# A two-layer decoder trunk: layer 1's adaLN vectors as row sums on VectorE over transposed weights

## The chip, the cores and the metric

The kernel runs on one core of a Trainium2 chip. The metric is the device time of one execution in microseconds (us), as the median of several runs. The core's engines are named as in its profile: PE (TensorE matmul), PEld (TensorE weight load), DVE (VectorE), ACT (ScalarE), POOL (GpSimd), and SP, whose queue issues nearly all DMAs.

## The reference

Two layers work on x of 256 tokens by 2048 features, in float32. Layer 0 mixes with a convolution module, layer 1 with differential attention; each is followed by a squared-ReLU MLP of width 8192. Each layer is steered by six vectors of 2048, the adaLN vectors, that come from one conditioning vector c:

```python
cond = jax.nn.silu(c)                            # (1, 2048)
for i in range(2):
    mod = cond @ ada_w[i] + ada_b[i]             # ada_w[i]: (2048, 6 * 2048)
    sh_m, sc_m, g_m, sh_f, sc_f, g_f = jnp.split(mod, 6, axis=-1)
    h = x * (1.0 + sc_m) + sh_m
    y = conformer_conv(h, ...) if i == 0 else diff_attention(h, ...)
    x = layer_norm(alpha * x + g_m * y, ln_mix_g[i], ln_mix_b[i])
    h = x * (1.0 + sc_f) + sh_f
    y = jnp.square(relu(h @ mlp_w1[i] + mlp_b1[i])) @ mlp_w2[i] + mlp_b2[i]
    x = layer_norm(alpha * x + g_f * y, ln_ffn_g[i], ln_ffn_b[i])
```

The weights `ada_w` are two matrices of 2048 by 12288 floats, 201 MB together, each element used once.

## The kernel before, in words

All large products are done in tiles of 512 output columns. A weight tile `w` of 1 MB (4 blocks of 128 rows by 512 columns) comes by one DMA from SP's queue into a ring of four buffers (`wraw`, tag "raw"). In two halves of 128x1024, ACT rounds it to fp32r (`wh`, line 629) and DVE takes the rest (`wl`, line 631); each 128x512 block of weights is then multiplied three times for each of two token halves on PE (lines 669, 671 and 672). A weight tile is thus 24 matmuls, two ACT casts and two DVE subtractions. ACT, DVE, PE and SP each work their queue in order, so a late `wl` stops PE, and a DVE instruction that waits holds up every `wl` behind it.

The adaLN vectors that this change touches are the last 12 of 16 column blocks of layer 0's last vector (`G_F`, gate of the MLP) and all six of layer 1. They are made during layer 0's MLP and layer 1, spread between weight tiles by `pump_slow`: a table `marks` says how many steps shall have been issued after so many weight tiles. The first 16 steps go between tiles 3 and 17, 66 more up to tile 122, some in the attention, 8 in the output projection `wo`, the last 8 at tiles 196 to 207.

A step (`ada_steps`, line 373) loads 128 rows of `ada_w` by 2048 columns (1536 for layer 0's) into a buffer of the same ring as the weight tiles, and DVE adds it, times one cond value for each partition, to the accumulator `acc` (lines 377 and 379). After 16 steps, `acc` holds 128 partial sums for each column. Four steps of the order's clock (`SUM_WAIT`) later PE adds them over the partitions with a block of ones (line 387, `adps`: four matmuls, three for layer 0's), ACT copies the result (line 390, `adrow`), PE turns it into columns with four transposes (line 396, `adpt`), and DVE adds the bias (line 399) into `mod`, which is 128 partitions by 16.

Layer 0's `G_F` is wanted soon after: `gate_bcast` turns `mod` into rows on PE (`gbm_p`), writes them to DRAM (`gbm_d`) and reads them back over all partitions (`gbm`, 1 MB), for the first product `w2g` on DVE (line 839) in the MLP's second matrix.

The pools of the early part are closed (`close_early`) about when the first step is issued; `acc` lies in a pool, `late`, that opens there. The order within each engine is set by a scheduler that goes by priorities, with a hand-made order on some engines in the early part.

Of the kernel before, what the change touches and what calls it, by code (L numbers as in the profile page):

```python
# [29 lines left out]
DEPTH = 2  # L30
# [11 lines left out]
ADA_MLP = 66  # L42
ADA_WO = 8
# [7 lines left out]
M2 = (196, 207)  # L51
M1 = (3,17)
# [3 lines left out]
ACT_Q = (0,2)  # L56
SUM_WAIT = 4
COL_WAIT = 1
POOL_T2 = ((5,),(2,5),(2,5),())
# [9 lines left out]
SH_M, SC_M, G_M, SH_F, SC_F, G_F = range(6)  # L69
# [4 lines left out]
MAGIC = 1.5 * 2.0 ** 23  # L74
PI_IN = 3.1415925


@with_exitstack
def trunk(
# [19 lines left out]
    late = {}  # L99
# [4 lines left out]
    def tp_tile(name):  # L104
        return ps_tp[0].tile([P, 512], F32, tag="tp", name=name)
# [65 lines left out]
    def defer(n, fn):  # L171
        put_off.append((ticks[0] + n, fn))
# [14 lines left out]
    adab = []  # L187
# [178 lines left out]

    def ada_steps(i, v, q0=0, m=None):

        st = {}
        c0, nr = q0 * NG, 32 * (4 - q0)  # L370

        def step(kc):
            w = wraw.tile([P, 2048], F32, tag="raw", name=f"adaw_{i}_{v}_{kc}")[:, c0:]
            nc.sync.dma_start(w, ada_w[i, kc * P:(kc + 1) * P, v * D + c0:(v + 1) * D])
            if kc == 0:
                st["acc"] = late["pool"].tile([P, D], F32, tag="acc", name=f"acc_{i}_{v}")[:, c0:]
                nc.vector.tensor_scalar(st["acc"], w, cond[:, 0:1], None, ALU.mult)
            else:
                nc.vector.scalar_tensor_tensor(  # L379
                    st["acc"], w, cond[:, kc:kc + 1], st["acc"], ALU.mult, ALU.add)  # L380
            if kc == KC - 1:
                st["m"] = m or mod_tile(i, v)

                def sums():
# [4 lines left out]
                    rows = work.tile([P, NG], F32, tag="bc_b2", name=f"adrow_{i}_{v}", bufs=1)  # L389
                    nc.scalar.copy(rows[:nr, :], ps[:nr, :])  # L390
                    defer(COL_WAIT, lambda: columns(rows))

                def columns(rows):
                    pt = tp_tile(f"adpt_{i}_{v}")
                    for j in range(4):
                        nc.tensor.transpose(out=pt[:, j * P:j * P + nr], in_=rows[:nr, j * P:(j + 1) * P],
                                            identity=ident[:nr, :nr])
                    for q in range(q0, 4):
                        nc.vector.tensor_tensor(st["m"][:, 4 * q:4 * q + 4],
                                                pt.rearrange("p (j n) -> p j n", j=4)[:, :, 32 * (q - q0)],  # L400
                                                adab[i][:, v * KC + 4 * q:v * KC + 4 * q + 4], op=ALU.add)
                    mods[(i, v)] = st["m"]
                defer(SUM_WAIT, sums)
        return [lambda kc=kc: step(kc) for kc in range(KC)]


# [1434 lines left out]
```

## Time and profile before

| | us |
|---|---|
| median of 3 runs | 2349.42 |
| lowest and highest run | 2344.43 and 2352.29 |
| span of the profiled execution, first to last instruction | 2342.9 |
| PE busy in that span | 2279.1 (97%) |
| DVE busy | 1743.6 (74%) |
| ACT busy | 1089.7 (47%) |
| DMA | 606.50 MB, mean 259 GB/s |

The profiled execution's own time is known by its span alone; what lies around the span is not listed. The span is 1.5 us below the lowest of the three runs and 6.5 us below their median. Busy time on PE counts a matmul that waits inside its pipeline as well, so that 97% is not 97% of PE's best; how close its instructions start behind one another tells more.

### The profile page before, as it was taken

To read this page: it belongs to the slowest core of one execution; us is meant where nothing else is said; L and a number is where in the kernel's file an instruction comes from. 1 tells how busy PE (TensorE), PEld (TensorE's weight loads), DVE (VectorE), ACT (ScalarE), POOL (GpSimd) and SP (SyncE) were. 2 spreads that over 40 slices of the span, in tenths; PEclk is the share of its full clock that TensorE was granted. 3 is DMA by queue.
4 is the path that set the end of the run, shared out by engine and by line. 5 is a ranking of instruction groups with operands and counts; after the bars stand their busy time and mean duration, and the time that the engine had idled before them with its cause. 6 is when DMAs were issued, how large, how long until landed. Compare 5 with 4: busy or idle time off the path is not lost.

```text
span 2342.9 us, 28838 instructions
## 1 busy us (share of the span) xinstructions
PE 2279.1 (97%) x11265; PEld 1809.2 (77%) x11265; DVE 1743.6 (74%) x2031; ACT 1089.7 (47%) x1503; POOL 149.4 (6%) x110
## 2 busy tenths in 40 slices
PE   7999989999999999999999999999999999999999
PEld 4676647777788888888878888877888888888886
DVE  5787788878887888877878876887975655655566
ACT  3344674365345445445454454545443443443442
POOL 0000002002200000000004200010220000000000
PEclk9999999999999999999999999999999999999999
DMA  9998489869988888888847655784876565555563
GB/s 342 377 341 295 164 314 376 316 221 329 326 315 308 312 290 307 308 301 291 310 163 269 242 201 195 256 319 162 305 247 202 180 197 191 187 186 193 189 223 108
DMA packets 264721, 606.50 MB, mean 259 GB/s; under 512 B 11137, under 2 KB 24583, under 8 KB 251527
## 3 DMA queue, kind: packets, MB, share of 16 engines
q1 hardware_dynamic: 264472, 604.62, 73.9%
q8 instruction: 88, 1.44, 0.3%
q14 instruction: 49, 0.39, 0.0%
q10 hardware_dynamic: 112, 0.05, 0.0%
HBM read 602.48 MB, written 2.15 MB: 258 GB/s over the span
## 4 chain that ended last, share of the span: by engine, by line
PE 74%; issue 16%; DVE 6%; ACT 2%; DMA 2%; POOL 0%; POOLq 0%; ACTq 0%; DVEq 0%; SPq 0%
PE w_ps L669 18%; PE w_ps L671 18%; PE w_ps L672 18%; DVE wl_w L631 1%; DMA w_w<-in_mlp_w_dram 1%; PE pw_ps L669 1%; PE qkv_v_ps L672 1%; PE qkv_v_ps L669 1%; PE qkv_v_ps L671 1%; PE qkv_q_ps L672 1%; PE qkv_q_ps L669 1%; DVE acc L379 1%; PE qkv_q_ps L671 1%; PE pw_ps L671 1%; PE pw_ps L672 1%
## 5 line engine op out<-in xcount | busy, mean ns | idle before, releaser
L631 DVE TENSOR_TENSOR wl_w<-w_w,wh_w 128x1024 fp32r<-128x1024 f32 x510 | 633.3, 1259 | 340.0 <-ACT wh_w L629 339.3
L629 ACT CAST wh_w<-w_w 128x1024 fp32r<-128x1024 f32 x512 | 537.0, 1054 | 703.4 <-PE w_ps L672 563.9
L669 PE MATMUL w_ps<-wh_w,hm_hi 128*128 128x512 f32 x1024 | 402.3, 393 | 3.0 <-ACT hm_hi L490 3.0
L671 PE MATMUL w_ps<-wl_w,u_hi 128*128 128x512 f32 x1024 | 399.4, 390 | 4.1 <-DVE wl_w L631 4.1
L671 PE MATMUL w_ps<-wl_w,hm_hi 128*128 128x512 f32 x1024 | 399.5, 390 | 2.5 <-DVE wl_w L631 2.5
L672 PE MATMUL w_ps<-wh_w,hm_lo 128*128 128x512 f32 x1024 | 399.3, 390 | 1.6 <-DVE hm_lo L493 1.6
L669 PE MATMUL w_ps<-wh_w,u_hi 128*128 128x512 f32 x1024 | 400.6, 391 | 0.0
L672 PE MATMUL w_ps<-wh_w,u_lo 128*128 128x512 f32 x1024 | 399.1, 390 | 0.0
L379 DVE SCALAR_TENSOR_TENSOR acc<-adaw,cond,acc 128x2048 f32<-128x2048 f32 (+1 forms) x105 | 244.5, 2329 | 0.1
L669 PEld LDWEIGHTS w_ps<-wh_w,hm_hi 128*128 128x128 f32 x1024 | 192.5, 188 | 47.5 <-ACT hm_hi L490 4.5
L671 PEld LDWEIGHTS w_ps<-wl_w,u_hi 128*128 128x128 f32 x1024 | 192.4, 188 | 45.3 <-DVE wl_w L631 5.8
L671 PEld LDWEIGHTS w_ps<-wl_w,hm_hi 128*128 128x128 f32 x1024 | 192.5, 188 | 43.4 <-DVE wl_w L631 4.6
L672 PEld LDWEIGHTS w_ps<-wh_w,hm_lo 128*128 128x128 f32 x1024 | 192.4, 188 | 43.0 <-DVE hm_lo L493 3.1
L669 PEld LDWEIGHTS w_ps<-wh_w,u_hi 128*128 128x128 f32 x1024 | 192.6, 188 | 42.0 <-issue 1.7
L672 PEld LDWEIGHTS w_ps<-wh_w,u_lo 128*128 128x128 f32 x1024 | 192.5, 188 | 40.2
L580 PE MATMUL pw_ps<-wh_pw,h_hi 128*128 128x512 f32 x256 | 105.7, 413 | 9.4 <-DVE sums L1122 3.3
L581 PE MATMUL pw_ps<-wl_pw,h_hi 128*128 128x512 f32 x256 | 101.5, 397 | 5.1 <-DVE wl_pw L569 5.1
L582 PE MATMUL pw_ps<-wh_pw,h_lo 128*128 128x512 f32 x256 | 100.8, 394 | 0.0
L569 DVE TENSOR_TENSOR wl_pw<-w_pw,wh_pw 128x1024 fp32r<-128x1024 f32 x64 | 77.5, 1220 | 21.2 <-ACT wh_pw L568 21.2
L568 ACT CAST wh_pw<-w_pw 128x1024 fp32r<-128x1024 f32 x64 | 65.8, 1050 | 41.6 <-PE pw_ps L582 24.5
L580 PEld LDWEIGHTS pw_ps<-wh_pw,h_hi 128*128 128x128 f32 x256 | 48.5, 190 | 39.5 <-issue 16.1
L581 PEld LDWEIGHTS pw_ps<-wl_pw,h_hi 128*128 128x128 f32 x256 | 48.7, 190 | 15.9 <-DVE wl_pw L569 7.2
(375 smaller groups left out, 3147.4 us busy)
## 6 DMA issues: line engine op xcount, KB each, us to landing
w_w<-in_mlp_w_dram SPq DMA_DIRECT2D x256, 1024.0 KB, 5.4
adaw<-in_ada_w_dram SPq DMA_DIRECT2D x96, 1024.0 KB, 5.6
aw<-in_ada_w_dram SPq DMA_DIRECT2D x40, 1024.0 KB, 7.3
w_pw<-in_conv_pw_w_dram SPq DMA_DIRECT2D x64, 512.0 KB, 9.1
conv_ux<-in_ada_w_dram SPq DMA_DIRECT2D x17, 1024.0 KB, 12.9
w_pw<-in_conv_pw_w_dram SPq DMA_DIRECT2D x16, 1024.0 KB, 9.2
w_qkv_q<-in_attn_qkv_w_dram SPq DMA_DIRECT2D x16, 1024.0 KB, 5.4
w_qkv_k<-in_attn_qkv_w_dram SPq DMA_DIRECT2D x16, 1024.0 KB, 5.2
```

What stands on the lines that cost most here:

```text
L379: nc.vector.scalar_tensor_tensor(st["acc"], w, cond[:, kc:kc + 1], st["acc"], ALU.mult, ALU.add)
L568: nc.scalar.copy(hq, rq)
L569: nc.vector.tensor_tensor(lq, rq, hq.bitcast(F32), op=ALU.subtract)
L580: nc.tensor.matmul(pss[t], lhsT=xh, rhs=wh, start=(kc == first), stop=False)
L581: nc.tensor.matmul(pss[t], lhsT=xh, rhs=wl, start=False, stop=False)
L582: nc.tensor.matmul(pss[t], lhsT=xl, rhs=wh, start=False, stop=(kc == last))
L629: nc.scalar.copy(hi, rq)
L631: eng.tensor_tensor(lo, rq, hi.bitcast(F32), op=ALU.subtract)
L669: nc.tensor.matmul(pss[tt], lhsT=xh, rhs=wh, start=(kc == 0 and job["bias"] is None), stop=False)
L671: nc.tensor.matmul(pss[tt], lhsT=xh, rhs=wl, start=False, stop=False)
L672: nc.tensor.matmul(pss[tt], lhsT=xl, rhs=wh, start=False, stop=(kc == nk - 1))
```

## The change

The weights of these vectors are laid out anew, transposed and in chunks, before the kernel is launched: a new input `ada_rows` holds, for each column block `ch`, a chunk of 128 output columns by 2048 inputs. A step now loads one chunk (1 MB, one piece of memory, rows of 8 KB) and makes 128 finished values with one DVE instruction: chunk times cond, summed along the row into one column of `mod`. For that, cond must lie on every partition as a row of 2048: it is computed once more in row form at the start (`cond_r`, 16x128, one ACT and one DVE instruction), written to DRAM (`cond_mem`, from ACT's queue), and read back to all partitions (`cond_rows`, 1 MB) when the pool `late` opens, in the place that `acc` had. The product is written over the chunk in place. Layer 0's part is 12 steps of 2048 wide in place of 16 of 1536; the others keep 16 steps. The sums, copies and transposes (lines 387, 390 and 396), both waits, and the bias adds in fours go; one bias add for each vector stays.

```diff
+ADA_ROWS = {key: n for n, key in enumerate([(0, G_F, ch) for ch in range(4, KC)] + [
+    (1, v, ch) for v in range(6) for ch in range(KC)])}
...
+    cond_r = work.tile([P, P], F32, tag="S", name="cond_r", bufs=3)[:KC, :]
+    nc.scalar.activation(cond_r, c_rows, AF.Sigmoid)
+    nc.vector.tensor_tensor(cond_r, cond_r, c_rows, op=ALU.mult)
+    cond_mem = dram.tile([KC, P], F32, tag="cond", name="cond_mem")
+    nc.scalar.dma_start(cond_mem, cond_r)
...
-        def step(kc):
-            w = wraw.tile([P, 2048], F32, tag="raw", name=f"adaw_{i}_{v}_{kc}")[:, c0:]
-            nc.sync.dma_start(w, ada_w[i, kc * P:(kc + 1) * P, v * D + c0:(v + 1) * D])
-            if kc == 0:
-                st["acc"] = late["pool"].tile([P, D], F32, tag="acc", name=f"acc_{i}_{v}")[:, c0:]
-                nc.vector.tensor_scalar(st["acc"], w, cond[:, 0:1], None, ALU.mult)
-            else:
-                nc.vector.scalar_tensor_tensor(
-                    st["acc"], w, cond[:, kc:kc + 1], st["acc"], ALU.mult, ALU.add)
...
-                    ps = tp_tile(f"adps_{i}_{v}")
-                    for q in range(q0, 4):
-                        nc.tensor.matmul(ps[32 * (q - q0):32 * (q - q0) + 32, :], lhsT=ones[:, 0:32],
-                                         rhs=st["acc"][:, q * NG - c0:(q + 1) * NG - c0], start=True, stop=True)
...
+        def step(ch):
+            w = wraw.tile([P, D], F32, tag="raw", name=f"adaw_{i}_{v}_{ch}")
+            nc.sync.dma_start(w, ada_rows[ADA_ROWS[i, v, ch]])
...
+            nc.vector.scalar_tensor_tensor(w, w, 1.0, late["cond"], ALU.mult, ALU.mult,
+                                           accum_out=st["m"][:, ch:ch + 1])
+            if ch == KC - 1:
+                mf = st["m"][:, ch0:]
+                nc.vector.tensor_tensor(mf, mf, adab[i][:, v * KC + ch0:(v + 1) * KC], op=ALU.add)
...
+        late["cond"] = late["pool"].tile([P, D], F32, tag="acc", name="cond_rows")
+        with tc.issue_after(raws["dma"].ins):
+            nc.sync.dma_start(late["cond"], cond_mem.rearrange("k p -> (k p)").partition_broadcast(P))
...
-        marks = ((0, 0), (M1[0], 0), (M1[1], 16), (122, 16 + ADA_MLP), (133, 16 + ADA_MLP))
+        marks = ((0, 0), (M1[0], 0), (M1[1], 12), (122, 12 + ADA_MLP), (133, 12 + ADA_MLP))
```

Three places show what moves. The first is PE at the end of a layer-1 vector in layer 0's MLP; `w_0_1_2_ps` is the sum of a weight tile's product. Before:

```order
L672 MATMUL w_0_1_2_ps_5864<-wh_w_0_1_2_2_1_5925,hm_lo 128x512
L387 MATMUL adps_1_5997<-acc_1_4930,ones 32x512 x4
L669 MATMUL w_0_1_2_ps_5863<-wh_w_0_1_2_3_0_5947,hm_hi 128x512
L671 MATMUL w_0_1_2_ps_5863<-wl_w_0_1_2_3_0_5948,hm_hi 128x512
```

Now:

```order
L656 MATMUL w_0_1_2_ps_5845<-wh_w_0_1_2_2_1_5906,hm_lo 128x512
L653 MATMUL w_0_1_2_ps_5844<-wh_w_0_1_2_3_0_5928,hm_hi 128x512
L655 MATMUL w_0_1_2_ps_5844<-wl_w_0_1_2_3_0_5929,hm_hi 128x512
L656 MATMUL w_0_1_2_ps_5844<-wh_w_0_1_2_3_0_5928,hm_lo 128x512
```

The sums are gone, and so are the transposes at seven like places; the order of the instructions that stay on PE is the same.

The second place is SP's queue where the first steps are issued. Before:

```order
L618 DMA w_w_0_0_1_0_4221<-in_mlp_w_dram 128x4x512
L374 DMA adaw_5_0_4253<-in_ada_w_dram 128x1536
L374 DMA adaw_5_1_4257<-in_ada_w_dram 128x1536
L618 DMA w_w_0_0_1_1_4272<-in_mlp_w_dram 128x4x512
L374 DMA adaw_5_2_4300<-in_ada_w_dram 128x1536
```

Now:

```order
L602 DMA w_w_0_0_1_0_4226<-in_mlp_w_dram 128x4x512
L379 DMA adaw_5_4_4260<-in_ada_rows_dram 128x2048
L1475 DMA cond_rows<-cond_mem 128x2048
L602 DMA w_w_0_0_1_1_4275<-in_mlp_w_dram 128x4x512
L379 DMA adaw_5_5_4303<-in_ada_rows_dram 128x2048
```

The read of `cond_rows`, which takes no buffer of the ring, stands where the second step's load stood.

The third place is SP's queue at the start of layer 0's second MLP matrix, where the gate `gbm` is read back. Before:

```order
L787 DMA gbm_d<-gbm_r 16x128
L374 DMA adaw_1_2_5070<-in_ada_w_dram 128x2048
L825 DMA basem_d<-basem_r 16x128
L618 DMA w_w_0_0_1_2_5085<-in_mlp_w_dram 128x4x512
L788 DMA gbm_4986<-gbm_d 128x2048
L618 DMA w_w_0_0_1_3_5123<-in_mlp_w_dram 128x4x512
```

Now:

```order
L771 DMA gbm_d<-gbm_r 16x128
L379 DMA adaw_1_2_5051<-in_ada_rows_dram 128x2048
L809 DMA basem_d<-basem_r 16x128
L772 DMA gbm_4967<-gbm_d 128x2048
L602 DMA w_w_0_0_1_2_5066<-in_mlp_w_dram 128x4x512
L602 DMA w_w_0_0_1_3_5104<-in_mlp_w_dram 128x4x512
```

The gate's read has moved ahead of one weight tile's load.

## Rows read from the trace of the kernel before

**Rows 1.** From the page: PE's busy time, share and instructions, and PE's granted clock in 40 equal slices of the span, in tenths.

```profile
PE 2279.1 (97%) x11265; PEld 1809.2 (77%) x11265; DVE 1743.6 (74%) x2031; ACT 1089.7 (47%) x1503; POOL 149.4 (6%) x110
...
PEclk9999999999999999999999999999999999999999
```

**Rows 2.** The table by stage: from and to, length, busy time of PE, PEld, DVE, ACT and POOL with the number of instructions, granted clock, DMA share, GB/s.

```profile
500.00:560.00 60.00, 57.93 (x264) 47.23 (x263) 49.28 (x35) 33.27 (x59) 11.90 (x6) 1.00 0.89 316
560.00:620.00 60.00, 55.75 (x245) 43.51 (x244) 47.37 (x39) 26.46 (x38) 14.25 (x6) 0.97 0.90 329
620.00:1195.00 575.00, 575.00 (x2604) 473.20 (x2603) 459.30 (x435) 269.80 (x362) 6.52 (x4) 1.00 0.85 303
...
1275.00:1525.00 250.00, 249.46 (x1163) 204.94 (x1162) 191.21 (x271) 126.66 (x231) 38.90 (x39) 1.00 0.66 225
1525.00:1600.00 75.00, 73.20 (x325) 59.65 (x325) 62.33 (x70) 31.81 (x42) 6.32 (x4) 1.00 0.80 284
...
1640.00:1715.00 75.00, 74.55 (x349) 60.50 (x348) 69.89 (x60) 34.30 (x40) 18.52 (x8) 1.00 0.89 303
```

**Rows 3.** The timeline of PE around one vector's sums and transposes: start, time, engine, line, operation.

```profile
725.53 0.39 PE L672 MATMUL w_ps<-wh_w,hm_lo 128*128 128x512 f32 x1
725.85 1.07 PE L387 MATMUL adps<-acc,ones 128*32 128x512 f32 x8
726.84 0.50 PE L669 MATMUL w_ps<-wh_w,hm_hi 128*128 128x512 f32 x1
727.18 0.39 PE L671 MATMUL w_ps<-wl_w,hm_hi 128*128 128x512 f32 x1
...
729.47 0.39 PE L672 MATMUL w_ps<-wh_w,hm_lo 128*128 128x512 f32 x1
729.71 0.60 PE L396 MATMUL adpt<-ident,adrow 128*128 128x128 f32 x4
...
730.37 0.40 PE L671 MATMUL w_ps<-wl_w,hm_hi 128*128 128x512 f32 x1
```

**Rows 4.** The chain of work that ended last, in order of time (start, time, what): the pieces of the sums, six in all, of which the first and the last.

```profile
725.91 1.00 PE adps L387 x8
...
1701.65 1.00 PE adps L387 x8
```

**Rows 5.** Groups of instructions on DVE and ACT, forms apart: line, engine, operation, out<-in, shapes, count, busy us, mean ns of one, idle before.

```profile
L379 DVE SCALAR_TENSOR_TENSOR acc<-adaw,cond,acc 128x2048 f32<-128x2048 f32 x90 | 214.2, 2380 | 0.0
L377 DVE TENSOR_SCALAR acc<-adaw,cond 128x2048 f32<-128x2048 f32 x6 | 7.7, 1282 | 4.0 <-PE adps L387 4.0
L399 DVE TENSOR_TENSOR mod<-adpt,cols_adab 128x4 f32<-128x4 f32 x27 | 2.5, 152 | 1.7 <-PE adpt L396 1.7
L1457 DVE SCALAR_TENSOR_TENSOR r<-r 128x512 f32<-128x512 f32 x32 | 22.2, 692 | 1.1
L1772 DVE SCALAR_TENSOR_TENSOR z<-z,lnf_rs,fin 128x512 f32<-128x512 f32 x5 | 3.8, 752 | 0.2
...
L1653 ACT ACTIVATION_READ_ACCUMULATOR at_sm<-at_sm,at_mx 128x1 f32 x32 | 6.0, 187 | 0.0
```

**Rows 6.** The table by stage, for the instructions of line 379 alone: from and to, length, DVE busy with the number of instructions, granted clock, DMA share, GB/s.

```profile
620.00:1195.00 575.00, 135.85 (x58) 1.00 0.85 303
...
1640.00:1715.00 75.00, 20.83 (x8) 1.00 0.89 303
```

**Rows 7.** The chain of work that ended last: the pieces of the steps, 13 of line 379, of which the first and the last, and the one of line 377.

```profile
509.27 0.53 DVE acc L379
...
582.57 1.20 DVE acc L377
...
1688.66 2.26 DVE acc L379
```

**Rows 8.** The timeline of DVE and of PE around the gate's read (in brackets the idle time before and what ended it), and the table by stage for the same place.

```profile
600.21 0.69 DVE L839 TENSOR_TENSOR w2g<-w_ps,gbm 128x512 f32<-128x512 f32 x1 [5.43 <-DMA gbm<-gbm_d]
...
603.01 1.22 DVE L631 TENSOR_TENSOR wl_w<-w_w,wh_w 128x1024 fp32r<-128x1024 f32 x1
...
604.28 0.50 PE L671 MATMUL w_ps<-wl_w,u_hi 128*128 128x512 f32 x1 [2.40 <-DVE wl_w L631]
...
609.79 0.50 PE L671 MATMUL w_ps<-wl_w,u_hi 128*128 128x512 f32 x1 [1.28 <-DVE wl_w L631]
...
604.00:612.00 8.00, 6.44 (x22) 4.71 (x23) 8.00 (x6) 1.04 (x1) 4.66 (x2) 0.79 0.82 264
```

**Rows 9.** The DMA issues (KB each, median us from issue to landing) of the two reads over all partitions that have one, SP's queue and DVE at the first steps, and a stretch with the DMA engines full.

```profile
conv_ux<-gb_d SPq DMA_DIRECT2D x1, 1024.0 KB, 12.5
gba<-gba_d SPq DMA_DIRECT2D x1, 1024.0 KB, 6.6
...
471.23 14.16 SPq L374 DMA_DIRECT2D adaw<-in_ada_w_dram  x2
...
493.68 1.01 DVE L377 TENSOR_SCALAR acc<-adaw,cond 128x1536 f32<-128x1536 f32 x1
...
572.00:580.00 8.00, 7.61 (x37) 5.09 (x36) 3.85 (x5) 7.57 (x14) 0.00 (x0) 1.00 1.01 375
```

**Rows 10.** The timeline of PE: behind the sums of layer 0's vector, and at the start of the kernel.

```profile
576.03 0.50 PE L671 MATMUL w_ps<-wl_w,u_hi 128*128 128x512 f32 x1 [0.39 <-DVE wl_w L631]
...
7.45 1.94 PE L327 MATMUL aps_b<-aw_bNone,condr 128*32 128x256 f32 x16 [4.34 <-DMA aw_bNone<-in_ada_w_dram]
```

More of the change, by code (lines that the diff above doesn't have):

```diff
@@ L56 @@
 ACT_Q = (0,2)
-SUM_WAIT = 4
-COL_WAIT = 1
 POOL_T2 = ((5,),(2,5),(2,5),())
@@ L84, in trunk @@
     conv_pw2_w, conv_pw2_b, attn_qkv_w, attn_lq1, attn_lk1, attn_lq2, attn_lk2,
-    attn_subln_g, attn_o_w, mlp_w1, mlp_b1, mlp_w2, mlp_b2, inv_freq, out,
+    attn_subln_g, attn_o_w, mlp_w1, mlp_b1, mlp_w2, mlp_b2, inv_freq, ada_rows, out,
 ):
@@ L365, in ada_both_steps, with ada_steps @@
         return la, lb, [lambda a=a: step(a) for a in range(n_pairs)], finish
-    def ada_steps(i, v, q0=0, m=None):
+    def ada_steps(i, v, ch0=0, m=None):
         st = {}
-        c0, nr = q0 * NG, 32 * (4 - q0)
-        def step(kc):
-            w = wraw.tile([P, 2048], F32, tag="raw", name=f"adaw_{i}_{v}_{kc}")[:, c0:]
-            nc.sync.dma_start(w, ada_w[i, kc * P:(kc + 1) * P, v * D + c0:(v + 1) * D])
-            if kc == 0:
-                st["acc"] = late["pool"].tile([P, D], F32, tag="acc", name=f"acc_{i}_{v}")[:, c0:]
-                nc.vector.tensor_scalar(st["acc"], w, cond[:, 0:1], None, ALU.mult)
-            else:
-                nc.vector.scalar_tensor_tensor(
-                    st["acc"], w, cond[:, kc:kc + 1], st["acc"], ALU.mult, ALU.add)
-            if kc == KC - 1:
-                st["m"] = m or mod_tile(i, v)
-                def sums():
-                    ps = tp_tile(f"adps_{i}_{v}")
-                    for q in range(q0, 4):
-                        nc.tensor.matmul(ps[32 * (q - q0):32 * (q - q0) + 32, :], lhsT=ones[:, 0:32],
-                                         rhs=st["acc"][:, q * NG - c0:(q + 1) * NG - c0], start=True, stop=True)
[L389 to L404, printed above, removed]
@@ new lines, in step @@
+        def step(ch):
+            w = wraw.tile([P, D], F32, tag="raw", name=f"adaw_{i}_{v}_{ch}")
+            nc.sync.dma_start(w, ada_rows[ADA_ROWS[i, v, ch]])
+            if ch == ch0:
+                st["m"] = m or mod_tile(i, v)
+            nc.vector.scalar_tensor_tensor(w, w, 1.0, late["cond"], ALU.mult, ALU.mult,
[3 more added lines that the diff above has]
+                nc.vector.tensor_tensor(mf, mf, adab[i][:, v * KC + ch0:(v + 1) * KC], op=ALU.add)
+                mods[(i, v)] = st["m"]
@@ L407, in trunk @@
+        return [lambda ch=ch: step(ch) for ch in range(ch0, KC)]
     ada_q, items, n_items, limit, after_load = [], [], [0, 0], [5], []
@@ L466, in trunk @@
     gf_load, gf_use = ada_slice_steps(0, G_F, 0, 4, m_gf, apart=True)
-    ada_q.extend(ada_steps(0, G_F, 1, m_gf))
+    ada_q.extend(ada_steps(0, G_F, 4, m_gf))
     for iv in [(1, SC_M), (1, SH_M), (1, G_M), (1, SC_F), (1, SH_F), (1, G_F)]:
@@ L1488, in close_early @@
         late["pool"] = ctx.enter_context(tc.tile_pool(name="late", bufs=1))
-    n_ada0 = 7 * KC
+        late["cond"] = late["pool"].tile([P, D], F32, tag="acc", name="cond_rows")
+        with tc.issue_after(raws["dma"].ins):
+            nc.sync.dma_start(late["cond"], cond_mem.rearrange("k p -> (k p)").partition_broadcast(P))
+    n_ada0 = 6 * KC + 12
     tiles_done = [0]
@@ L1496, in pump_slow @@
         n = tiles_done[0]
-        marks = ((0, 0), (M1[0], 0), (M1[1], 16), (122, 16 + ADA_MLP), (133, 16 + ADA_MLP))
+        marks = ((0, 0), (M1[0], 0), (M1[1], 12), (122, 12 + ADA_MLP), (133, 12 + ADA_MLP))
         left = 80 - ADA_MLP
         for g in range(4):
-            marks += ((133 + 12 * g, 96 - left * (4 - g) / 4), (137 + 12 * g, 96 - left * (3 - g) / 4))
-        marks += ((177, 96), (185, 96 + ADA_WO), (M2[0], 96 + ADA_WO), (M2[1], 112), (1000, 112))
+            marks += ((133 + 12 * g, 92 - left * (4 - g) / 4), (137 + 12 * g, 92 - left * (3 - g) / 4))
+        marks += ((177, 92), (185, 92 + ADA_WO), (M2[0], 92 + ADA_WO), (M2[1], 108), (1000, 108))
         want = np.interp(n, [m[0] for m in marks], [m[1] for m in marks])
@@ L1830 @@
         -np.arange(0, HD, 2, dtype=np.float32) / np.float32(HD))).astype(np.float32)
-    for name in _INS + ["inv_freq"]:
+    aw = [np.asarray(inputs["ada_w"])[i].T.reshape(6, KC, P, D) for i in range(DEPTH)]
+    inputs["ada_rows"] = np.stack([aw[i][v, ch] for i, v, ch in ADA_ROWS])
+    for name in _INS + ["inv_freq", "ada_rows"]:
         a = np.ascontiguousarray(inputs[name])
```

## The prediction

> **What bounds the kernel now.** I began with the page: PE is busy for 2279.1 of 2342.9 us, at the full granted clock in nearly every slice [rows 1]. So an instruction that leaves PE can shorten the kernel, but only in stages where PE itself ends last, and the mean doesn't tell which these are. Hence the table by stage [rows 2]. From 620 to 1195 us PE is busy for all 575.0 us, DVE for 459.3 and the DMA engines for 0.85: PE bounds. From 1275 to 1525 PE has 249.46 of 250. From 500 to 620 it lacks 2.07 and 4.25 us, with DMA at 0.89 and 0.90: there weights and their splitting come late now and then. From 1640 to 1715 PE has 74.55 of 75, but DVE 69.89, so that DVE has only 5.1 us to spare. The seven vectors' sums fall on 574, 726, 865, 1013, 1154, 1490 and 1702 us: four in the first kind of stage, one in the second, one at 574 in the third, one in the last. Then the chain that ended last: it holds six pieces "adps" of 1.0 us each, all but the one at 574 [rows 4], and 13 pieces of the steps' DVE work [rows 7], in the stages where DVE runs close.
>
> **The change part by part.** *The sums and transposes on PE.* What they cost is not their busy time, since matmuls overlap, but by how much they push the next one back. Without anything between them, the matmuls of a tile start 0.23 us apart. Around the sums, from the start of the last matmul before them (725.53) to the second one behind (727.18), 1.65 us pass where two distances would be 0.46: they cost 1.19 us. Around the transposes 729.47 to 730.37 is 0.90, and they cost 0.44 [rows 3]. That is 1.63 us for a vector, and six vectors on the chain give 6 x 1.63 = 9.8 us. Of these the four between 620 and 1195 (6.5 us) are the safest: DVE and DMA there have room for a PE that is 1.1% faster. The seventh (three sums, 574 us) lies where PE, once through them, waits for `wl` anyway, 0.39 us before 576.03 [rows 10]; I count its transposes alone, 0.4 us, between 0 and 1.6.
>
> *The other removed work.* Seven ACT copies and 27 bias adds of 152 ns [rows 5] stand where ACT and DVE have idle time, or are replaced by seven adds. I count 0; in no stage would they be worth more than the adds of one vector, 0.6 us.
>
> *The steps on DVE.* Before: 90 steps of 2380 ns, 15 narrower ones, and 7 first steps, of which the wide ones take 1282 ns as a one-input product [rows 5]. After: 108 alike, all 2048 wide with two inputs. Layer 0's part takes as long in 12 wide steps as in 16 narrow ones, since the elements are the same. A step's price changes by two things. Its scalar is a constant, not a column read from memory: the same operation over 512 elements takes 692 ns with a constant and 752 with a column [rows 5], so 60 ns come off. And it must write out a sum, which the trace doesn't show on DVE. The nearest row is ACT's separate read of its accumulator, 187 ns; the lower bound is 0, for a sum written within the instruction. I take 110 ns, a small DVE instruction in the shadow of its neighbour being nearer to the bias add's 152 than to 187. So a step changes by +50 ns, between -60 and +130. Over 108 steps that is 5 us of DVE time, hidden nearly everywhere; on the chain lie 13 pieces of steps, so +0.7 us (-0.8 to +1.7). The first step of a vector grows by 1282 to 2430 ns, and one of these seven is on the chain, at 582.57 [rows 7]: +1.1. Together +1.8 us, between +0.3 and +2.8. A wait on its own sum is no issue: each step writes another column, and DVE works in order.
>
> [...]
>
> *The row of cond.* At the start one ACT and one DVE instruction and an 8 KB write on ACT's queue are added. PE's first sums wait 4.34 us for a DMA there, until 7.45 [rows 10], and `cond_r` needs well under 1 us: nothing. Later the read over 128 partitions, 1.05 MB, comes into the stage with the fullest DMA queues. At the 375 GB/s that the trace shows with all engines busy [rows 9] it takes 2.8 us of them. Two such reads took 6.6 and 12.5 us to land [rows 9]. SP reaches it where the second step's load stood, between 471.23 and 485.4, when SP was held by a full ring [rows 9]; this read needs no buffer of the ring, but the end of the early pools' last readers. It lands between 478 and 498, and the first step ran at 493.68 [rows 9]. So DVE may stand up to 4 us before its first step, and queued behind that are the two `wl` of the next weight tile, for which PE waits. Against it: the load of the next weight tile moves one place nearer in the ring, and the ring serves 12 chunks rather than 16 between tiles 3 and 17. I take +1.0 us, between -1 and +7 (4.2 for the wait and 2.8 for the traffic).
>
> *The gate of layer 0's MLP.* [...] Now the read of `gbm` is ahead of one weight tile's load, 2.8 us of traffic, in a queue where both wait for one another. `gbm` comes up to 2.8 us earlier, and PE's stall of 2.40 could go, with the clock's fall behind it; the weight tile comes later by as much and can stop PE itself. I take -2.0 us, between -5.4 and +2.
>
> *Sum.* -9.8 - 0.4 + 1.8 + 1.0 - 2.0 = -9.4 us on the profiled execution, whose span is 2342.9: 2333.5. That span is 6.5 us under the median of the runs, of which the lowest is 1.5 above it; I take the difference as staying, so 2349.4 - 9.4 = 2340.0 us. All good ends together give 2332; all bad ones, with the four safest vectors alone, -6.5 + 2.8 + 7 + 2 = +5.3, 2355.
>
> **The rivals.** *The gain is given back before 620 us.* The read of `cond` delays the first step, the weight tiles behind it come late, the gate's read makes a weight tile late, and the clock falls once more (1.7 us). With +5 for the first, +1 for the gate and 1.7 for the clock, in place of +1.0 and -2.0, the sum is -9.4 + 8.7 = -0.7: 2348.7. For it: 500 to 620 us is where DMA is at 0.9 and the chain goes through DMA, ACT and DVE. Against it: PE lost only 6.3 us there in all, and the ring has four chunks fewer. A milder form, with half of this, gives 2344; both are within 0.3%, which is 7.0 us and about what a measurement of this kernel can tell from no change.
>
> *A step with a running sum is dear on DVE.* This one ends slower. [...] It decides from about 0.75 us a step on: 13 pieces on the chain times 0.75 are the 9.8 us that PE wins. For it: nothing in the trace shows a sum on DVE. [...]
>
> *That the change doesn't do what it says* can be excluded for PE: its order has lost the sums and transposes and nothing else.
>
> **How the numbers follow.** The forecast has 0.64, the gain given back 0.25, the dear step 0.11. Within the forecast a little (0.07) lies closer than 0.3%, when only the four safest vectors pay; of the second, 0.02 end over 0.3% slower. So faster 0.57, the same 0.30, slower 0.13. The likeliest time is 2340. The range leaves out the dear step (0.11) and the far ends: 2333, all good ends nearly, to 2350, the gain given back and a little scatter of the runs.
>
> **What would show it right or wrong.** Right: no `adps` and `adpt` on PE; 620 to 1195 us shorter by 6.5 us, with PE still all busy; the steps on DVE within 0.15 us of 2380 ns, a short extra instruction included; `w2g` waiting less for `gbm`, and no granted clock under 1.00 about there. Wrong: a step of 3 us or more and DVE near 100% from 620 to 1195; DVE idle before its first step for the read of cond; PE waiting for `wl` between 485 and 620 by more than the 6.3 us of before; or the stages behind 620 us no shorter, with the matmuls further apart than 0.23 us.

## The result, and the profile after

| | us |
|---|---|
| before, median of 4 runs | 2350.68 (2344.43 to 2352.29) |
| after, median of 4 runs | 2330.55 (2329.77 to 2334.33) |
| ratio after to before | 0.9925, 95% interval 0.9909 to 0.9941 |
| span of the profiled execution, before and after | 2342.9 and 2327.4 |
| own time of after's profiled execution | 2329.99 |

After is faster, and by more than forecast: 2330.55 us lies 9.5 us under the predicted 2340 and under the lower end of the range, 2333. The two profiles differ by 15.5 us, where the sum had 9.4.

Busy times on the page of after, which answer to [rows 1]. PE has 11.2 us less, DVE as much as before:

```profile
PE 2267.9 (97%) x11183; PEld 1807.8 (78%) x11183; DVE 1744.0 (75%) x2116; ACT 1085.6 (47%) x1497; POOL 148.7 (6%) x110
```

The table by stage of after, for [rows 2] and the last row of [rows 8]. The stage behind the gate ends 15 us earlier now, so its row runs from 613.5 to 1180.

```profile
500.00:560.00 60.00, 60.00 (x276) 49.87 (x275) 53.76 (x44) 34.47 (x60) 15.52 (x8) 1.00 0.95 340
560.00:620.00 60.00, 57.46 (x255) 46.29 (x254) 47.70 (x48) 27.97 (x38) 7.03 (x5) 1.00 0.91 331
604.00:612.00 8.00, 8.00 (x37) 6.64 (x36) 8.00 (x8) 2.01 (x2) 0.00 (x0) 1.00 0.88 262
613.50:1180.00 566.50, 566.39 (x2547) 469.43 (x2546) 456.99 (x482) 266.62 (x357) 10.24 (x6) 1.00 0.87 308
```

From 500 to 560 us PE lacks nothing, where it lacked 2.07; at 604 to 612 the granted clock is 1.00, where it was 0.79. Behind the gate PE is busy throughout, as forecast.

PE's timeline of after at the place of the first sums of [rows 3], between the same weight tiles; one matmul starts 0.23 us behind the other:

```profile
718.02 0.39 PE L655 MATMUL w_ps<-wl_w,hm_hi 128*128 128x512 f32 x1
718.25 0.39 PE L656 MATMUL w_ps<-wh_w,hm_lo 128*128 128x512 f32 x1
718.47 0.39 PE L653 MATMUL w_ps<-wh_w,hm_hi 128*128 128x512 f32 x1
```

The steps on DVE, first as groups of after (the answer to [rows 5]), then DVE's timeline of after, then two rows of DVE's timeline of before:

```profile
L382 DVE SCALAR_TENSOR_TENSOR adaw<-adaw,cond_rows 128x2048 f32<-128x2048 f32 x108 | 249.9, 2314 | 0.5 <-DMA adaw<-in_ada_rows_dram 0.5
L382 DVE DVE_READ_ACCUMULATOR adaw<-adaw,cond_rows 128x1 f32 x108 | 8.8, 81 | 0.0
```

```profile
692.80 2.28 DVE L382 SCALAR_TENSOR_TENSOR adaw<-adaw,cond_rows 128x2048 f32<-128x2048 f32 x1
695.01 0.08 DVE L382 DVE_READ_ACCUMULATOR adaw<-adaw,cond_rows 128x1 f32 x1
695.01 1.22 DVE L615 TENSOR_TENSOR wl_w<-w_w,wh_w 128x1024 fp32r<-128x1024 f32 x1
```

```profile
700.09 2.35 DVE L379 SCALAR_TENSOR_TENSOR acc<-adaw,cond,acc 128x2048 f32<-128x2048 f32 x1
702.35 1.22 DVE L631 TENSOR_TENSOR wl_w<-w_w,wh_w 128x1024 fp32r<-128x1024 f32 x1
```

The sum costs an instruction of 81 ns, but the next one starts with it. From a step's start to the next start 2.21 us pass, where 2.26 passed before.

DVE's timeline of after at the gate, for the first rows of [rows 8]. `w2g` waits for PE's product, no longer for `gbm`:

```profile
593.47 0.69 DVE L823 TENSOR_TENSOR w2g<-w_ps,gbm 128x512 f32<-128x512 f32 x1 [2.72 <-PE w_ps L656]
```

Where the time went is seen best from something that each kernel does in the same order: the 736 `wh` roundings on ACT. The table has the times between the starts of the 1st, 101st, 176th, 357th, 451st, 491st and 541st, in us, read from each kernel's profile. The second stage is the one with layer 0's part and the gate. The third holds the sums of four vectors, the fourth (the attention) those of the fifth, the fifth is the output projection with its 8 steps, and the sixth has the last vector.

| kernel | to 482 | to 698 | to 1223 | to 1508 | to 1635 | to 1778 |
|---|---|---|---|---|---|---|
| before | 465.7 | 216.3 | 525.5 | 284.5 | 127.6 | 142.8 |
| before again | 467.3 | 215.9 | 525.5 | 286.9 | 129.2 | 142.8 |
| after | 465.8 | 209.1 | 518.6 | 283.3 | 127.7 | 142.2 |
| layer 0 only | 465.9 | 213.7 | 525.5 | 284.4 | 129.8 | 142.9 |
| layer 1 only | 466.0 | 213.0 | 518.6 | 282.7 | 127.7 | 142.1 |
| sums back | 466.0 | 209.9 | 525.5 | 286.3 | 129.0 | 142.6 |
| gate early | 466.2 | 215.7 | 525.5 | 284.5 | 127.7 | 142.9 |
| sixteen loads | 466.5 | 216.7 | 518.6 | 283.4 | 129.3 | 142.1 |
| longer steps | 465.8 | 213.7 | 520.5 | 291.4 | 132.6 | 146.5 |
| wider marks | 466.2 | 209.7 | 520.1 | 283.0 | 127.5 | 140.0 |
| last steps wider | 466.6 | 209.1 | 518.6 | 284.5 | 127.4 | 140.2 |
| none in wo | 466.2 | 212.3 | 520.6 | 283.0 | 125.1 | 140.5 |
| all early | 464.8 | 213.9 | 523.2 | 284.5 | 125.1 | 140.0 |
| later denser | 465.8 | 209.0 | 521.3 | 284.8 | 127.0 | 140.0 |

After against before: 7.2 us less in the second stage, 6.9 in the third, 1.2 in the fourth and 0.6 in the sixth, 0.1 more in the first and the fifth: together 15.7 us, the difference of the spans but for 0.2. Each row is one execution. The third and the sixth column repeat to 0.3 us among kernels that are alike there; the first, the fourth and the fifth scatter by 2 to 3 us (see before and before again), so that the 1.2 in the fourth says little by itself.

### The profile page after: what moved, and what is told of

Same layout as the page of the kernel before. It is cut to its first block, busy times and chain, and to the rows that moved or that the text cites. A ratio compares the mean times of both kernels' runs of the same rounds, so it can differ in the third digit from the quotient of the medians.

```text
span 2327.4 us, 28629 instructions
## 1 busy us (share of the span) xinstructions
PE 2267.9 (97%) x11183; PEld 1807.8 (78%) x11183; DVE 1744.0 (75%) x2116; ACT 1085.6 (47%) x1497; POOL 148.7 (6%) x110
## 4 chain that ended last, share of the span: by engine, by line
PE 74%; issue 16%; DVE 6%; ACT 2%; DMA 2%; POOL 0%; POOLq 0%; DVEq 0%; ACTq 0%; SPq 0%
PE w_ps L656 18%; PE w_ps L655 18%; PE w_ps L653 18%; DVE wl_w L615 2%; PE pw_ps L653 1%; PE qkv_q_ps L656 1%; PE qkv_q_ps L653 1%; PE qkv_q_ps L655 1%; PE qkv_v_ps L656 1%; PE qkv_v_ps L653 1%; PE qkv_v_ps L655 1%; PE ut L1425 1%; PE pw_ps L656 1%; DVE adaw L382 1%; PE pw_ps L655 1%
## 5 line engine op out<-in xcount | busy, mean ns | idle before, releaser
L382 DVE SCALAR_TENSOR_TENSOR adaw<-adaw,cond_rows 128x2048 f32<-128x2048 f32 x108 | 249.9, 2314 | 0.5 <-DMA adaw<-in_ada_rows_dram 0.5
```

What stands on the lines that cost most here:

```text
L382: nc.vector.scalar_tensor_tensor(w, w, 1.0, late["cond"], ALU.mult, ALU.mult, accum_out=st["m"][:, ch:ch + 1])
```

## Experiments

Theory A at the start of them: the gain has two sources, the work that left PE (third stage on) and, ahead of that, fewer loads in the ring and an earlier gate. Rival B: PE's work is all, and the rest is scatter.

Each kernel was run beside before. In this section a difference in us between the times of two kernels is worked out from their ratios, times before's median beside them; it isn't the difference of two medians in this text. The 95% interval of a ratio stands in brackets.

**Layer 0's part alone by the new way.** `ada_steps_old` makes the steps, sums and transposes as in before.

```diff
-        ada_q.extend(ada_steps(*iv))
+        ada_q.extend(ada_steps_old(*iv))
```

> Layer 0's last vector by the new way (12 wide chunks, row of cond), layer 1's six by the old way with sums on PE; the gate's read stands behind the weight tile's load, as in before. Theory A (the gain before 656 us comes from two things, the 12 chunks that take fewer places in the ring, and the gate's earlier read): about 2 to 4 us faster than before, made before 580 us, PE's waits for wl between 500 and 580 gone; the stall for the gate near 600 us stays; behind 620 us nothing changes. Rival B (only the sums on PE count, the rest of the difference is the usual scatter of one profile): not over 1 us faster.

Measured: 2345.64 us, ratio 0.9985 (0.9976 to 0.9993), so 3.5 us less than before. In the profile 2.6 of them lie in the second stage. Its table by stage, and its `w2g`:

```profile
500.00:560.00 60.00, 59.98 (x277) 49.58 (x276) 52.85 (x44) 34.98 (x60) 14.05 (x8) 1.00 0.93 337
604.00:612.00 8.00, 5.51 (x17) 4.26 (x17) 8.00 (x6) 2.09 (x2) 3.19 (x2) 0.79 0.98 352
```

```profile
597.11 0.69 DVE L864 TENSOR_TENSOR w2g<-w_ps,gbm 128x512 f32<-128x512 f32 x1 [5.44 <-DMA gbm<-gbm_d]
```

With 12 chunks PE loses 0.02 us from 500 to 560, and the stall at the gate with the lower clock behind it is still there. That is theory A's first half by itself, with one thing mixed in: layer 0's own sums and transposes have left PE as well, for which the prediction had 0.4 us.

**Layer 1 alone by the new way.** Layer 0's vector keeps `acc` (1536 columns wide); `cond_rows` gets a place of its own.

```diff
-    ada_q.extend(ada_steps(0, G_F, 4, m_gf))
+    ada_q.extend(ada_steps_old(0, G_F, 1, m_gf))
```

> Layer 1's six vectors by the new way, layer 0's by the old one (16 narrow steps and its sums on PE); the row of cond has a place of its own and the gate's read stands ahead of the weight tile's load, as in after. Theory A: 10 to 12 us faster than before (six vectors at 1.63 less about 1 for the last one, so 8.2 to 9.8, and 2 to 3 for the gate), the stage from 490 to 580 us as in before or worse. Rival B: the whole gain of after, 15 us or more.

Measured: 2336.65 us, ratio 0.9949 (0.9938 to 0.9961): 12.0 us less. The table by stage:

```profile
500.00:560.00 60.00, 57.40 (x263) 47.02 (x262) 49.58 (x35) 32.70 (x58) 12.88 (x6) 1.00 0.90 316
604.00:612.00 8.00, 8.00 (x36) 6.35 (x35) 8.00 (x7) 2.86 (x3) 3.54 (x2) 1.00 0.89 322
```

The mirror image: with 16 narrow steps PE loses 2.60 us from 500 to 560, but PE's stall behind the gate and the lower clock are gone. `w2g` itself still waits 2.88 us for `gbm`, where it waited 5.43. The third stage is after's to 0.1 us. The two halves add up, 0.15% and 0.51% to 0.66%, with after at 0.75% (0.59 to 0.91). Rival B falls.

**The sums put back on PE, for nothing.**

```diff
+        ps = tp_tile(f"adps_{i}_{v}")
+        for q in range(4):
+            nc.tensor.matmul(ps[32 * q:32 * q + 32, :], lhsT=ones[:, 0:32],
+                             rhs=late["cond"][:, q * NG:(q + 1) * NG], start=True, stop=True)
...
+        nc.scalar.copy(rows, ps)
...
+            nc.tensor.transpose(out=pt[:, j * P:(j + 1) * P], in_=rows[:, j * P:(j + 1) * P],
```

> After, with four 32x512 sums of the cond row on PE, the ACT copy and four transposes put back behind each vector of layer 1; nobody uses their results. Theory A: 8 to 9.8 us slower than after (1.63 us for each of six vectors, the last one less where DVE bounds), so still 5 us or more faster than before. Rival B: 13 us or more slower than after, nearly the time of before. Rival D (a matmul more costs nothing because PE has gaps in its pipeline): under 3 us.

Measured: 2341.44 us, ratio 0.9967 (0.9955 to 0.9979); against after's ratio that is 0.42%, 9.9 us. PE's timeline at the first of them:

```profile
719.50 0.39 PE L674 MATMUL w_ps<-wh_w,hm_lo 128*128 128x512 f32 x1
719.82 1.07 PE L394 MATMUL adps<-cond_rows,ones 128*32 128x512 f32 x8
720.81 0.50 PE L671 MATMUL w_ps<-wh_w,hm_hi 128*128 128x512 f32 x1
721.15 0.39 PE L673 MATMUL w_ps<-wl_w,hm_hi 128*128 128x512 f32 x1
```

From 719.50 to 721.15 it is 1.65 us as in [rows 3], and the third stage is back at before's 525.5: four vectors cost 6.9 us, 1.73 each. The second stage stays at 209.9, so that part of the gain has nothing to do with PE's sums in layer 1. Theory A.

**Before, with the gate's read ahead of one weight tile's load.** Nothing of the new way is in it.

```diff
-                raws["dma"] = nc.sync.dma_start(...)
+                with tc.issue_after(raws["gate"].ins) if name == "w2_0_0_1_2" else ExitStack():
+                    raws["dma"] = nc.sync.dma_start(...)
```

> Before, with one thing moved: the load of the weight tile that stood ahead of the gate's read stands behind it; the new way is in no part of it. Theory A: 2 to 5 us faster than before (the stalls of 2.40 and 1.28 us near 600 us and the fall of the clock behind them go). Rival B: within 1 us of before; or the weight tile, later by 2.8 us, stops PE instead and it is no faster.

Measured: 2344.94 us, ratio 0.9977 (0.9967 to 0.9987): 5.4 us less. The table by stage:

```profile
500.00:560.00 60.00, 55.60 (x254) 44.88 (x252) 45.02 (x34) 31.89 (x58) 10.18 (x6) 1.00 0.86 304
604.00:612.00 8.00, 6.97 (x31) 5.46 (x30) 8.00 (x5) 4.11 (x4) 3.57 (x2) 1.00 1.00 361
```

The clock stays full and PE's loss at the gate shrinks from 1.56 to 1.03 us in the second row; its profile loses 4.40 us from 500 to 560 instead, more than before's 2.07, so that in this one execution the second stage is only 0.6 us shorter. The runs say that the gate's place is worth something by itself, 5.4 us (by the interval 3 to 8); this profile, of an execution of 2345.86 us, doesn't show where.

**The 12 chunks in 16 loads.** Blocks 4, 7, 10 and 13 come in two halves, the bytes stay; the gate's read stays early, by the edit just shown, as in all kernels from here on but the longer steps and before again.

```diff
+            w = wraw.tile([P, D], F32, tag="raw", name=f"adaw_{i}_{v}_{ch}_{h}")[:, :1024]
+            nc.sync.dma_start(w, ada_rows[ADA_ROWS[i, v, ch]][:, 1024 * h:1024 * h + 1024])
...
-    n_ada0 = 6 * KC + 12
+    n_ada0 = 7 * KC
```

> After, with layer 0's 12 chunks loaded as 16 pieces: four of the chunks (blocks 4, 7, 10 and 13) come as two halves of 1024 inputs each, so the bytes and the elements on DVE are the same and four more places of the ring are taken between tiles 3 and 17; the gate's read stays ahead of the weight tile's load. Theory A1 (it is the number of ring places that delays the weight tiles): PE loses 2 to 4.5 us again between 500 and 560 us, as in before and the two kernels with 16 narrow steps, and the time is 2 to 4.5 us over after. Rival A2 (the bytes or the DVE time of the steps, or the sums): PE loses under 0.5 us there and the time is within 1 us of after.

Measured: 2340.39 us, ratio 0.9956 (0.9944 to 0.9968), 0.31% or 7.3 us over after. The second stage is 7.6 us longer than after's, the third is the same. The table by stage:

```profile
500.00:560.00 60.00, 56.95 (x254) 46.12 (x252) 45.26 (x44) 31.39 (x57) 11.52 (x6) 0.97 0.88 305
560.00:620.00 60.00, 56.35 (x242) 45.45 (x243) 52.04 (x51) 27.46 (x38) 7.97 (x5) 0.97 0.94 342
```

PE loses 3.05 us in the first row, as the kernels with 16 narrow steps do (2.07 to 4.40), and in both rows the granted clock falls under 1.00, as it did at the gate in before. Bytes and DVE elements are the same; a few short DVE instructions come along, but DVE is busy for 45.26 of 60 us there, less than in after. So it is the number of loads, each of which takes a place in the ring (A1, and more than A1 had, by the clock). SP's queue shows how such a loss arises (start, time), in before, in after and in this kernel:

```profile
513.73 0.50 SPq L795 DMA_DIRECT2D basem_gb<-in_ln_mix_g_dram  x1
515.02 3.99 SPq L374 DMA_DIRECT2D adaw<-in_ada_w_dram  x2
520.42 0.38 SPq L618 DMA_DIRECT2D w_w<-in_mlp_w_dram  x1
```

```profile
513.60 0.50 SPq L779 DMA_DIRECT2D basem_gb<-in_ln_mix_g_dram  x1
515.37 0.33 SPq L379 DMA_DIRECT2D adaw<-in_ada_rows_dram  x1
518.00 2.59 SPq L602 DMA_DIRECT2D w_w<-in_mlp_w_dram  x2
```

```profile
516.05 3.67 SPq L392 DMA_DIRECT2D adaw<-in_ada_rows_dram  x2
520.54 0.76 SPq L622 DMA_DIRECT2D w_w<-in_mlp_w_dram  x1
...
532.17 0.38 SPq L622 DMA_DIRECT2D w_w<-in_mlp_w_dram  x1
```

In before two steps stand behind one another, and the next weight tile is issued when both have found a buffer, at 520.42. In after one step stands there, and two weight tiles follow from 518.00 on. With 16 loads of the wide chunks' bytes two steps stand there again, the next weight tile is issued at 520.54, and the one behind it at 532.17 only. PE's waits from 500 to 572 us follow the count: 2.1 to 5.2 us in the five kernels with 16 loads (before, before again, layer 1 only, gate early, sixteen loads), 0 to 0.2 in the four with 12 and the steps placed as in after (after, layer 0 only, sums back, last steps wider).

The longest single wait of PE in this kernel is not explained by that hold, since the weight tile that it goes back to was issued ahead of it, at 514.90. Here are ACT's and PE's rows:

```profile
524.32 1.04 ACT L633 CAST wh_w<-w_w 128x1024 fp32r<-128x1024 f32 x1 [6.39 <-DMA w_w<-in_mlp_w_dram]
525.27 1.06 ACT L1441 COPY us<-w_ps 128x512 f32<-128x512 f32 x2
...
525.90 1.14 PE L1447 MATMUL ut<-ident,us 128*128 128x128 f32 x8 [2.89 <-ACT us L1441]
```

ACT rounds the tile 9.4 us after its issue, where the same tile took 7.5 in after, and `us`, for which PE waits, stands behind it. The granted clock over 520 to 540 us is 0.91. Two steps' loads follow that tile at once, where one does in after; that they slow it is not shown. Another explanation of the whole loss would be that a chunk in one piece of memory lands sooner than a strided load. The few landings known from 480 to 575 us speak against it: in the median a narrow load of before took 6.3 us from issue to landing, a chunk of after 7.6, a half chunk here 6.1.

**Steps that are longer by one DVE instruction.** The extra one writes 512 columns of the chunk back unchanged.

```diff
+            nc.vector.scalar_tensor_tensor(w[:, :512], w[:, :512], 1.0, w[:, :512], ALU.mult, ALU.max)
```

> After, with one more DVE instruction of 512 columns (about 0.7 us, it writes the chunk's values back unchanged) ahead of each of the 108 steps: 75 us more of DVE work. By the working of the prediction, in which 13 pieces of the steps lie on the chain, this costs about 9 us. Theory A now (PE is busy throughout from 620 to 1195 us and DVE has 110 us to spare there, against 40 us more): nothing there, 2 to 4 us for the 18 steps before 620 us, 1 to 4 us for the 8 steps between 1640 and 1715, where DVE has 5 us to spare and 5.6 more come: 3 to 8 us in all. Rival: DVE is the hidden bound of the middle stage, 20 us or more.

Measured: 2351.11 us, ratio 1.0006 (0.9997 to 1.0014): 0.81%, 19 us, over after, for 108 x 0.69 = 75 us of DVE. Theory A expected 3 to 8 us and was wrong, and so was the rival, since the third stage takes 1.9 us only. It is the attention (8.1 us), the output projection (4.9), the second stage (4.6) and the sixth (4.3) that grow. PE's waits from 1260 to 1590 us (in total, times, longest), first in this kernel, then in after:

```profile
PE qkt_k L1611 <- DVE rp_k L1606: 4.5, 4, 1.6
PE at_a L1657 <- DVE at_sm L1650: 3.3, 2, 1.9
PE wo_ps L656 <- DVE wl_wo L616: 3.2, 2, 2.2
```

```profile
PE at_a L1656 <- DVE at_sm L1649: 1.6, 2, 1.1
PE wo_ps L655 <- DVE wl_wo L615: 1.5, 1, 1.5
```

The 22 steps there stand in DVE's queue ahead of work that PE wants at once (`rp_k`, the rotated keys): PE's waits come to 11.0 us, where they were 3.1. That most steps of after just pass is concluded from this, not shown by a run of its own.

**Wider marks.** The five steps of the order's clock that the sums and columns waited (`SUM_WAIT`, `COL_WAIT`) are given to the steps.

```diff
-M1 = (3,17)
+M1 = (3,19)
-M2 = (196, 207)
+M2 = (196, 210)
```

> After, with the time that the removed waits for sums and columns gave back put to use: layer 0's 12 steps are spread over tiles 3 to 19 rather than 17, the last 8 over tiles 196 to 210 rather than 207; the gate's read again ahead of the weight tile's load. Theory: DMA between 520 and 560 us no longer at 1.0, DVE no longer at 0.93 between 1640 and 1715: 1 to 2 us faster than after. Against it: the gate comes one or two tiles later and w2g waits for it, 2 to 5 us slower.

Measured: 2330.79 us, ratio 0.9919 (0.9907 to 0.9931), as after. The last stage is 2.2 us shorter, the second 0.6 and the third 1.5 us longer: half of the expectation holds.

**Before again.**

> Before, unchanged, once more with a profile: what differs between two executions of it. If the losses of PE between 500 and 560 us (2.07 us in the first profile), and the stall with the clock's fall near 600 us, belong to the program, they stand in this profile too, within 2 us; its span should be longer than 2342.9 us, since that profile was of one of the fastest executions, and the place of the difference shows what scatters.

Measured: 2351.0 us. The span by cores, and the table by stage:

```profile
core 0: 2349.2 us, clock 0.992
```

```profile
500.00:560.00 60.00, 57.79 (x264) 46.91 (x263) 49.60 (x36) 32.78 (x58) 11.88 (x6) 1.00 0.91 319
604.00:612.00 8.00, 5.92 (x18) 4.37 (x19) 8.00 (x5) 1.89 (x2) 5.07 (x2) 0.79 0.70 222
```

The losses at 500 to 560 (2.21 us) and at the gate (granted clock 0.79) belong to the program. Of the 6.3 us of span more than in the first profile 5.6 lie in the first, the fourth and the fifth stage and 1.3 behind the sixth, and the mean clock is 0.992, not 0.995: that is what scatters from run to run.

**The last steps wider, the rest as in after.**

```diff
-M2 = (196, 207)
+M2 = (196, 210)
```

> After, with the last 8 steps spread over tiles 196 to 210 rather than 207, possible because the last vector no longer waits for sums and columns; layer 0's part as in after. Theory (this stage is bound by DVE, so that the last vector's sums on PE were worth only 0.6 us there): PE's loss of 1.55 us between 1670 and 1690 us goes, 1 to 2 us faster than after. Rival (the steps only move and DVE is full later): within 0.5 us of after.

Measured: 2330.34 us, ratio 0.9918 (0.9904 to 0.9931). The table by stage at the end, first in this kernel, then in after:

```profile
1630.00:1730.00 100.00, 100.00 (x454) 82.43 (x453) 85.20 (x81) 44.95 (x52) 20.22 (x11) 1.00 0.83 291
```

```profile
1630.00:1730.00 100.00, 98.45 (x446) 80.73 (x445) 83.02 (x78) 44.37 (x52) 23.98 (x10) 1.00 0.82 283
```

PE's loss of 1.55 us there is gone and the sixth stage 2.0 us shorter, but the runs can't tell this kernel from after.

**No steps in the output projection, 74 up to tile 122.**

```diff
-ADA_MLP = 66
-ADA_WO = 8
+ADA_MLP = 74
+ADA_WO = 0
```

> As the kernel with the last 8 steps spread to tile 210, and the 8 steps of the output projection are made up to tile 122, in layer 0's MLP, so that this stage has 74 steps rather than 66 and the output projection none. Theory (a step is free where PE bounds and dear where DVE does, as the longer steps showed: 5.8 us for 5.5 us of DVE in the output projection, under 2 us for 40 us between 620 and 1195): the losses in the output projection (some 3.5 us between 1510 and 1570) go, 2 to 4 us faster than after. Rival: the denser steps bring DMA and DVE before 700 us to their limits, 1 to 4 us slower there.

Measured: 2333.26 us, ratio 0.993 (0.9917 to 0.9942). The output projection is 2.6 us shorter, as expected; the second stage is 3.2 and the third 2.0 us longer. PE's waits from 500 to 1180 us:

```profile
PE basem_p L808 <- DVE basem_c L806: 3.6, 1, 3.6
PE w_ps L656 <- DVE wl_w L616: 2.9, 3, 1.7
```

**All steps early.** 82 up to tile 122, none in the output projection or in layer 1's MLP.

```diff
-ADA_MLP = 66
-ADA_WO = 8
+ADA_MLP = 82
+ADA_WO = 0
```

> All steps but the 14 in the attention are made by tile 122: 82 steps in layer 0's MLP and none in the output projection or in layer 1's MLP. Theory: the losses of PE in the output projection and between 1670 and 1690 us both go, 3 to 5 us faster than after, if DVE (0.81 busy between 620 and 1180) and DMA (0.85) have the room for 16 steps more there, 38 us of DVE and 17 MB. Rival: the transfers come too late in layer 0's MLP, with DMA over 0.93, and PE waits there: as fast as after or slower.

Measured: 2334.33 us, ratio 0.9939 (0.9926 to 0.9951). The second and the third stage give back 9.4 us; the rival holds: from 700 to 900 us DMA is at 0.93 of its time, and PE waits 4.1 us for `wl` between 500 and 1180, where it waited 1.1 in after.

**The 8 moved steps only behind tile 27.** The rest is as in the kernel with 74 steps up to tile 122.

```diff
-        marks = ((0, 0), (M1[0], 0), (M1[1], 12), (122, 12 + ADA_MLP), (133, 12 + ADA_MLP))
+        marks = ((0, 0), (M1[0], 0), (M1[1], 12), (27, 12 + 66 * 10 / 105), (122, 12 + ADA_MLP), (133, 12 + ADA_MLP))
```

> As the kernel without steps in the output projection (74 steps up to tile 122, the last 8 up to tile 210), but with the steps up to tile 27 at the pace of after, so that the stage around the gate is as in after, and the 8 moved steps between tiles 27 and 122. Theory: the losses before 620 us (2.8 us over after, PE's wait for basem_p) do not come, the gains in the output projection (2.6 us) and between 1670 and 1690 us (1.9 us) stay: 3 to 4.5 us faster than after, 2326 to 2328 us. Rival: the denser steps cost 1.7 us each time DMA is short behind tile 27 as well: 1 to 2 us faster only.

Measured: 2334.28 us, ratio 0.9936 (0.9923 to 0.9949), not faster than after. The second stage is after's (209.0), and the third is 2.7 us longer: around 880 us, where DVE also makes the tables of sines for the attention, PE waits for `wl` once. PE's waits from 700 to 1180 us, of which after has none:

```profile
PE w_ps L656 <- DVE wl_w L616: 1.6, 1, 1.6
PE ut L1428 <- ACT us L1422: 0.2, 1, 0.2
```

They explain 1.8 of the 2.7 us.

None of these placements of the steps beats after.

## Why the prediction was too small

*The sums and transposes on PE: right, 9.8 us forecast.* The third stage is 6.9 us shorter where 6.5 were forecast: 518.6 in each of the four kernels without the sums that leave the stage's steps and their places as they are (after, layer 1 only, sixteen loads, last steps wider), and 525.5 in each of the five with them. The fifth vector gives some 1.7, by the means of the fourth column with the sums (285.3) and without (283.7, longer steps left aside), in a scatter of 2. The last one gives 0.6 rather than 1.63: it lies in the stage where DVE had 5 us to spare, so that a wait for DVE took the place of PE's work; with the steps there spread wider that wait went and the stage gave 2.0 more. Together about 9.

*The steps on DVE: +1.8 us forecast, no loss seen.* A step takes 2284 ns in the median and its sum 82, in the shadow of the next instruction; 2.21 us from start to start against 2.26. My middle value of +50 ns had the wrong sign, within its bounds. A vector's first step did grow, from 1282 to about 2284 ns; no run prices that alone.

*The dear step.* That rival is out: the running sum doesn't slow the step, at 2284 ns with it and 2346 without, in the median. Its chance stood on a step that is longer by 0.75 us or more, and no run shows the sum to do that: in the median the step is 62 ns shorter. What does stand out is the step with two sources against the product of one in [rows 5], 1282 ns for the same 2048 elements: it takes 1.8 times as long, with a sum or without.

*The price of a longer step.* Had the step been dear, I had its price too low. "13 pieces on the chain" times the growth made 0.75 us a step the point from which it decides; 0.69 us cost 19 us, so that by proportion, as an estimate, some 0.35 us would have eaten PE's 9.8. The chain counts the pieces that end last now, not those that come next.

*The row of cond: +1.0 forecast, nothing seen.* Its read was issued at 482.38 in after, and the first step ran at 493.50, 0.2 us sooner than in before.

*The ring: the step that failed.* The prediction held that layer 0's part "takes as long in 12 wide steps as in 16 narrow ones, since the elements are the same", gave 0 to it in the sum, and used the four chunks fewer only as an argument, in the term of cond and against the first rival. That holds for DVE's elements, but each load takes a place in a ring of four, whatever its width, and that was left out. With the gate late, 12 for 16 gave 2.6 us (layer 0's sums on PE, which went with it, had 0.4 in the forecast); with the gate early, going back to 16 loads of the same bytes cost 7.6 us in the second stage, 3.05 of it PE's idle time before 560 us, about 1.1 more of that to 620 than in after, and the rest the lower clock in both rows, which partly followed the wait whose cause stays open. The other two kernels with 16 loads and the early gate (layer 1 only, gate early) take 213.0 and 215.7 us in that stage, 3.9 and 6.6 more than after, with the clock at 1.00 from 500 to 620 us.

*The gate: -2.0 us forecast, mechanism right, size too small.* The far end of the bounds, -5.4, is what [rows 8] show of before's stall: 2.40 and 1.28 us of PE's waits, and 1.7 us for the clock, an estimate from 0.79 granted over 8 us (0.21 x 8), which is also the 1.7 of the first rival. The -2.0 itself was my choice between the ends; no run shows it. In the three kernels with the late read (before, before again, layer 0 only) `w2g` waits 5.4 to 6.2 us for `gbm`, and the granted clock over 604 to 612 us is 0.79; in the others it is 1.00 there (for all early only 0.97 over 560 to 620 is known), and `w2g` waits 0 to 3.3 us for `gbm`. In layer 1 alone the second stage is 3.3 us shorter with the 16 narrow steps still in it; with 12 loads the early read makes 4.6 (213.7 to 209.1); moving only the read took 5.4 us off the runs of before, that far end, though only 0.6 off the second stage of the one profile. Ring and gate together are worth 7.2 us in the profile where the prediction had 1.4 (seventh vector, cond and gate).

*From the span to the median.* I took the 6.5 us between before's span and its median as staying. They didn't: before's profile was of one of its fastest executions (a second one had a span of 2349.2). With four runs 7.8 us lie between its span and its median, in after 3.1. So 15.5 us of the 20.1 between the medians are in the spans, and 4.6 are this; the interval of the ratio, 13.9 to 21.4 us, holds both numbers.

*The rivals.* Nothing was given back before 620 us; that stage was the second source of the gain.

Open stays how much of the second stage's gain is the gate's and how much the ring's: the two work through the same queue, 2.6 and 3.3 us alone and 7.2 together.

## What to carry to other kernels

Where loads of two kinds share a ring in one queue, count the places they take, not only their bytes: four loads fewer of the same bytes were worth 2.6 to 7.6 us here, at the upper end as much as all the work that left the bounding engine in the stage behind it. Price a change of an engine that runs close by lengthening its instruction, not by counting its pieces on the present chain: that count was short by half. And measure the scatter of the kernel before by a second profile ahead of turning a span into a median.

## What the hardware showed that I had not expected

- A scalar_tensor_tensor of 128x2048 float32 with a running sum and a constant scalar is as fast as one without a sum and with a column as scalar: 2284 against 2346 ns in the median, and the separate read of the sum, 82 ns (71 to 88), costs nothing more, since the next instruction begins together with it. A product of one float32 source takes 1282 ns for the same elements [rows 5], 0.55 of the step of two.
- The clock's fall behind the gate went with PE's stall: where `w2g` waited 5.4 to 6.2 us for `gbm`, the granted clock was 0.79 over 604 to 612 us (before, before again, layer 0 alone), in before 0.50 from 606 to 609; with the read ahead it was 1.00 there, all early left aside. In four kernels with the early read it fell elsewhere ahead of 620 us, behind other waits of PE: to 0.97 over 500 to 560 us with 16 loads, and to 0.97 over 560 to 620 with these as well as with the longer steps, with none in wo and with all early.
